# All of w_down through seven half-size products, in a two-layer encoder trunk on one core

## The chip, the core and the metric

The kernel runs on one core of a Trainium2 chip. Its time is the device time of one execution in microseconds, as the median of the runs. The profile is of one execution of its own. In it TensorE (PE) multiplies, PEld is its weight load, VectorE (DVE), ScalarE (ACT) and GpSimd (POOL) do the element-wise work, and SyncE (SP) issues most DMAs.

## The reference, cut to what matters

There are 512 tokens of width 1024, in two layers. Each layer is a mixer of attention heads, added to the residual, and then a squared-ReLU MLP, added to the residual. A final RMS norm follows. All of it is float32.

```python
def squared_relu_mlp(h, w_up, w_down):            # h 512x1024, w_up 1024x4096, w_down 4096x1024
    return jnp.square(jax.nn.relu(h @ w_up)) @ w_down

def reference(...):
    for layer in range(2):
        h = rmsnorm(x, norm_mix[layer])
        x = x + (even_mixer(h, ...) if layer == 0 else odd_mixer(h, ...))
        x = x + squared_relu_mlp(rmsnorm(x, norm_mlp[layer]), w_up[layer], w_down[layer])
    return rmsnorm(x, norm_final)
```

## The kernel before

**Precision.** A float32 matrix is split into two parts for TensorE: `hi`, a copy in fp32r made by ScalarE, and `lo`, the remainder, which VectorE makes with one subtraction. A product of two matrices is then three matmuls (`mm3`): hi by hi, hi by lo, lo by hi. Each matmul has a 128x128 stationary operand, and moves up to 512 columns into one PSUM bank.

**Order of the work.** The program text only records operations. The class `Plan` then orders them with a list scheduler. It has its own table of costs and the number of buffers of every pool. On each engine it takes, of the operations that are ready, the one that was recorded first. Work inside `nc.urgent` counts as recorded 4000 places earlier. The result is a fixed order on each engine, and an engine never passes its own next instruction. All instructions carry the same line of the program in the profile (L230, the recorder), so groups are told by the names of tiles.

**The names.** `X` are the four residual tiles, 128 tokens by 1024. `u` are feature-major activations (hi and lo). `wr` is a raw piece of weights and `wh`, `wl` are its hi and lo parts. `mm` is a PSUM bank of a plain product. `ex` is a scratch tile of 512 columns.

**The MLP (`mlp`).** The hidden width of 4096 is 32 chunks of 128. `up_pair` makes two chunks of relu(h @ w_up): 2 pieces of w_up, 48 matmuls, and one VectorE operation per chunk (`ex<-mm,rstd`). `up_raw` squares them on ScalarE into tiles `sq` (`squares`). Chunks go in groups of eight, and three groups, 24 chunks, go through `seven_products`. That is Strassen's scheme in Winograd's form: the eight chunks of activations (512 tokens by 1024) are cut in halves of tokens and of chunks, and w_down (1024 by 1024) in halves of chunks and of columns. Seven half-size products, of 24 matmuls each, take the place of eight. Sums and differences of the halves are made on VectorE in place (`into`: `sq<-sq,sq`, and `rw<-rw,rw` on the raw weights). `acts` splits an activation block into `sh`, `sl`, and `weights` splits a weight block into two pairs `wh`, `wl`. The products go to the banks `pa` (`main`) and `pb` (`second`, `third`), and `add` adds the banks to `X`. Between the products the next group's `up_raw` is recorded.

The last eight chunks do it plainly. `up_split` makes hi and lo at once, and `add_proj` multiplies them, four chunks at a time, in 96 matmuls. Its second call has `last=True` and finishes the tokens of `X[0]` and `X[1]` before those of `X[2]` and `X[3]`.

**Buffers that matter here.** Pages `sh`, `sl` come from a ring of six (`hd`), so three products' activations fit. `wh`, `wl` come from a ring of eight, so two products' weights fit. `rw` comes from a ring of nine.

**The start.** SP loads `X[0]`, the gain of the first norm as a broadcast to 128 partitions, the identity, `X[1]`, three pieces of w_in, `X[2]` and `X[3]`. `norm_T` scales the rows (`ex<-X,sm,gain`), transposes them on TensorE (`tr`) and splits them. Then `v_proj` runs 192 matmuls for the values of layer 0. 60 dummy matmuls (`warm`) run first, and 12 more after the first token tile.

**After the first MLP.** `first_of_layer_1` loads weights for the values of layer 1 in two blocks of 256 columns, partly into `hd` pages. `norm_T` follows, and then `v_proj` with 192 matmuls of 256 columns.

Of the kernel before, what the change touches and what calls it, by code (L numbers as in the profile page):

```python
# [25 lines left out]
WARM = 60  # L26
WARM2 = 12
LAYER_0 = """v a0 f0 f1 a1 a2 f2 f3 a3 f4 f5 f6 b0 f7 b1 c0 c1 b2 c2 b3 c3 x of c4 c5 c6 oc c7"""
# [356 lines left out]
def trunk(ctx, tc, x, positions, norm_mix, norm_mlp, norm_final, w_in_ab, b_forget, rel_bias,  # L385
# [56 lines left out]

    def load_w(view, parts=None, place="w", raw_place="w"):


        n = int(np.prod(view.shape[1:]))
        if raw_place == "hd":
            raw = hp.tile([P, 1024], F32, tag="hd", name=nm("wr"))
        else:
            raw = wp.tile([P, 1024], F32, tag="wr", name=nm("wr"), bufs=2)  # L450
        if place == "hd":
# [71 lines left out]
    def norm_rows(xt, g, n):  # L523

        junk = otile()
        ss = small(1)
        nc.scalar.activation(junk.bitcast(BF16)[:, :n], xt, AF.Square, accum_out=ss)
        r = rstd_of(ss, n)
        pieces = []
        for c in range(0, n, S):  # L530
            m = min(S, n - c)
            t = etile()
            nc.vector.scalar_tensor_tensor(t[:, :m], xt[:, c:c + m], r, g[:, c:c + m], ALU.mult, ALU.mult)
            pieces.append(t)
        return pieces
# [19 lines left out]

    def norm_T_(X, g_row, g=None, after=None):

        g = gain(g_row, D) if g is None else g
        hT = [(utile(), utile()) for _ in range(NC // 2)]
        for t in range(NT):  # L560
            for h, piece in enumerate(norm_rows(X[t], g, D)):
                to_feature_major(piece, 4, hT[2 * h:2 * h + 2], t)
            if t == 0 and after is not None:
                after(hT)
        return [(hi[:, k], lo[:, k]) for hi, lo in hT for k in range(2)]
# [46 lines left out]

    def col_blocks(w, kc, col, n, places=None, raw_place="w"):


        if places is None:
            per = 1024 // n
            places = [(min(per, kc - c), "w") for c in range(0, kc, per)]
        of, c = {}, 0
        for k, place in places:  # L620
            b = load_w(rows(w, c, c + k, col, col + n), place=place, raw_place=raw_place)
# [193 lines left out]

    def seven_products(X, R, wd, k0):

# [28 lines left out]

        def product(banks, A, B, first):

            for i in range(4):
                for q in range(2):  # L850
                    a = tuple(h[:, i, q * P:(q + 1) * P] for h in A)
                    b = tuple(h[:, i % 2] for h in B[i // 2])
                    mm3(banks[q], a, b, first and i == 0, i == 3, skip_group_check=not first)

        def add(banks, row, col):
            for q in range(2):
                xs = X[2 * row + q][:, col * S:(col + 1) * S]
                nc.vector.tensor_tensor(xs, banks[q], xs, ALU.add)

# [12 lines left out]
        add(second, 1, 1)  # L872
        yield

        into(a21, a22, a21, SUB)
# [9 lines left out]
        yield  # L885

        into(b11, b21, b11, SUB)
        product(second, acts(a22), weights(b11), False)
        add(second, 1, 0)
        yield  # L890

        third = side()
        product(third, acts(a12), weights(b21), True)
        add(third, 0, 0)
        yield

        into(a21, a12, a21, SUB)
        product(main, acts(a21), weights(b22), False)
        add(main, 0, 1)
        yield  # L900

    def mlp(X, g_row, wu, wd, ahead=None):

# [35 lines left out]
        def squares():  # L939
            return [up.tile([P, 2, S], F32, tag="u", name=nm("sq")) for _ in range(4)]  # L940

        R = squares()
        for pr in range(4):
            up_raw(0, pr, R)
        for g in range(3):
            steps = seven_products(X, R, wd, 8 * g)
            nxt = squares() if g < 2 else None
            act = []
            for pr, n in enumerate((2, 2, 2, 1)):
                for _ in range(n):  # L950
# [7 lines left out]
            R = nxt  # L958
        nxt = up_split(3584)
        if ahead is not None:  # L960
            ahead()
        add_proj(X, act, 4, wd, 24)
        add_proj(X, nxt, 4, wd, 28, last=True)

# [16 lines left out]
    def first_loads():  # L981
        g0.append(gain(norm_mix[0:1, :], D))
        nc.sync.dma_start(ident, consts[:, O_ID:O_ID + P])

    def first_weights():
        early[0] = {1: col_blocks(w_in_ab, NC, 1280, 264, raw_place="hd")}

    early = {}
    X = load_x(xr, between={0: first_loads, 1: first_weights})
    def keep_warm(hT):  # L990
        a = hT[0][0][:, 0, 0:P]
        for _ in range(WARM2):
            nc.tensor.matmul(warm[:, 0:P], lhsT=a, rhs=a, start=True, stop=True)

    hT = norm_T(X, None, g=g0[0], after=keep_warm)

    early[0][0] = col_blocks(w_in_ab, NC, 1024, 256)
    vw, ftail = v_proj(w_in_ab, 1024, hT, extra=8, order=(1, 0), w=early[0])
# [115 lines left out]
    def first_of_layer_1():  # L1114
        early["v"] = [col_blocks(w_in_cd, NC, 1024, 256, [(4, "hd"), (4, "hd")]),
                      col_blocks(w_in_cd, NC, 1280, 256, [(4, "hd"), (2, "rd")])]

    mlp(X, norm_mlp[0:1, :], w_up[0], w_down[0], ahead=first_of_layer_1)


# [131 lines left out]
    def step(name):  # L1252
        nonlocal vw, cq, ck, cqT, ckT, KR, o, wq, wkv
        kind, i = name.rstrip("01234567"), int(name[-1]) if name[-1].isdigit() else None
        if kind == "v":
            first, last = early["v"]
            tail = col_blocks(w_in_cd[6 * P:], 2, 1280, 256, [(2, "rd")])
            vw, _ = v_proj(w_in_cd, 1024, hT, w={0: first, 1: lambda c: last(c) if c < 6 else tail(c - 6)})
        elif kind == "q":
# [68 lines left out]
    add_proj(X, oD[2:4], 2, w_out_cd, 6, last=True)  # L1328
    mlp(X, norm_mlp[1:2, :], w_up[1], w_down[1])

# [46 lines left out]
```

## Time and profile before

| what | value |
|---|---|
| device time, median of 3 runs | 1189.9 us (1189.68 to 1191.11) |
| the profiled execution, device time | 1191.89 us |
| its span | 1190.2 us |
| PE, DVE, ACT, POOL busy in the span | 98%, 73%, 50%, 14% |
| matmuls | 5962 |

The page gives the busy time and the number of instructions of each engine. Then it gives the span in 40 slices, the DMA queues, the chain of work that ended last, and groups of like instructions with their mean duration and the idle time before them. The windows view gives busy time by stretches, with the granted clock of TensorE (PEclk). The timeline gives single instructions with start and duration in microseconds. Consecutive matmuls overlap: each is shown longer than the distance to the next.

### The profile page before, as it was taken

To read this page: it belongs to the slowest core of one execution; us is meant where nothing else is said; L and a number is where in the kernel's file an instruction comes from. 1 tells how busy PE (TensorE), PEld (TensorE's weight loads), DVE (VectorE), ACT (ScalarE), POOL (GpSimd) and SP (SyncE) were. 2 spreads that over 40 slices of the span, in tenths; PEclk is the share of its full clock that TensorE was granted. 3 is DMA by queue.
4 is the path that set the end of the run, shared out by engine and by line. 5 is a ranking of instruction groups with operands and counts; after the bars stand their busy time and mean duration, and the time that the engine had idled before them with its cause. 6 is when DMAs were issued, how large, how long until landed. Compare 5 with 4: busy or idle time off the path is not lost.

```text
span 1190.2 us, 16361 instructions
## 1 busy us (share of the span) xinstructions
PE 1168.5 (98%) x5962; PEld 990.9 (83%) x5962; DVE 864.6 (73%) x1452; ACT 596.4 (50%) x1066; POOL 168.1 (14%) x303
## 2 busy tenths in 40 slices
PE   8999999999999999999999998999999999999997
PEld 8988888788888888887898987788888888888886
DVE  6547888685977877776755879778768778687645
ACT  5347777544443444444435756566644434344423
POOL 2216522100000000000003718022100000000000
PEclk9999999999999999999999999899999999999999
DMA  6533335443143241215332230782622413321221
GB/s 200 152 94 110 93 85 169 154 156 89 36 141 107 67 146 53 71 36 172 119 105 62 60 120 30 178 226 76 213 71 71 155 58 121 109 71 36 85 92 71
DMA packets 101088, 126.85 MB, mean 107 GB/s; under 512 B 5304, under 2 KB 71232, under 8 KB 101008
## 3 DMA queue, kind: packets, MB, share of 16 engines
q1 hardware_dynamic: 100768, 125.50, 34.5%
q8 instruction: 47, 0.77, 0.2%
q0 software_dynamic: 240, 0.31, 0.2%
q14 instruction: 33, 0.27, 0.1%
HBM read 112.12 MB, written 4.23 MB: 98 GB/s over the span
## 4 chain that ended last, share of the span: by engine, by line
PE 89%; DVE 4%; DMA 4%; ACT 1%; issue 1%; POOL 0%; SPq 0%; POOLq 0%; ACTq 0%; DVEq 0%
PE mm L230 60%; PE pa L230 11%; PE pb L230 8%; PE tr L230 4%; PE sc L230 3%; PE av L230 3%; DMA KH<-KH 1%; DVE u L230 1%; DVE wl L230 1%; DMA X<-in_x_dram 1%; DVE ex L230 1%; DVE k L230 1%; ACT wh L230 1%; DMA wr<-in_w_down_dram 1%; DMA wr<-in_w_in_cd_dram 0%
## 5 line engine op out<-in xcount | busy, mean ns | idle before, releaser
L230 PE MATMUL mm<-u,wh 128*128 128x512 f32 (+1 forms) x1524 | 466.6, 384 | 1.1 <-DVE u L230 1.0
L230 PEld LDWEIGHTS mm<-u,wh 128*128 128x128 f32 x1524 | 281.1, 189 | 53.0 <-DVE u L230 1.8
L230 PE MATMUL mm<-u,wl 128*128 128x512 f32 (+1 forms) x762 | 292.5, 384 | 0.0
L230 PE MATMUL mm<-wh,u 128*128 128x512 f32 (+4 forms) x1008 | 269.6, 349 | 1.3 <-DVE o L230 0.6
L230 DVE TENSOR_TENSOR wl<-wr,wh 128x1024 fp32r<-128x1024 f32 (+5 forms) x152 | 173.8, 1149 | 74.5 <-ACT wh L230 73.7
L230 ACT CAST wh<-wr 128x1024 fp32r<-128x1024 f32 (+5 forms) x152 | 149.6, 988 | 152.3 <-PE mm L230 73.5
L230 PEld LDWEIGHTS mm<-wh,u 128*128 128x128 f32 x1008 | 176.1, 190 | 21.4 <-DVE X L230 1.2
L230 PE MATMUL mm<-wl,u 128*128 128x512 f32 (+4 forms) x504 | 175.1, 348 | 0.9 <-DVE wl L230 0.8
L230 PEld LDWEIGHTS mm<-u,wl 128*128 128x128 f32 x762 | 143.8, 189 | 26.0 <-DVE wl L230 0.2
L230 ACT CAST wh<-rw 128x1024 fp32r<-128x1024 f32 x84 | 88.5, 1054 | 114.3 <-PE mm L230 54.0
L230 DVE TENSOR_TENSOR wl<-rw,wh 128x1024 fp32r<-128x1024 f32 x84 | 102.8, 1224 | 57.0 <-ACT wh L230 56.5
L230 PEld LDWEIGHTS mm<-wl,u 128*128 128x128 f32 x504 | 95.7, 190 | 10.4 <-DVE wl L230 1.4
L230 POOL TENSOR_TENSOR sm<-sm,mhalf 128x1 f32<-128x1 f32 x28 | 20.2, 721 | 458.3 <-DVE sm L230 458.3
L230 POOL TENSOR_SCALAR p<-p,sm 128x128 f32<-128x128 f32 (+1 forms) x96 | 53.6, 558 | 175.7 <-DVE sm L230 129.9
L230 DVE TENSOR_TENSOR X<-mm,X 128x512 f32<-128x512 f32 x80 | 54.4, 687 | 28.8 <-PE mm L230 28.5
L230 PE MATMUL pa<-wl,sh 128*128 128x512 f32 x192 | 74.7, 389 | 0.0
L230 PE MATMUL pa<-wh,sl 128*128 128x512 f32 x192 | 74.7, 389 | 0.0
L230 ACT ACTIVATE sq<-ex 128x512 f32<-128x512 f32 x48 | 30.3, 631 | 88.5 <-DVE ex L230 88.5
L230 PE MATMUL pa<-wh,sh 128*128 128x512 f32 x192 | 74.4, 389 | 0.0
L230 DVE SCALAR_TENSOR_TENSOR ex<-mm,rstd 128x512 f32<-128x512 f32 x64 | 44.1, 688 | 39.5 <-PE mm L230 34.5
L230 PE MATMUL tr<-ident,p 128*128 128x128 f32 x320 | 65.6, 280 | 5.0 <-POOL p L230 3.5
L230 PE MATMUL av<-pt,u 128*128 128x128 f32 (+3 forms) x256 | 65.6, 340 | 0.0
(133 smaller groups left out, 1674.3 us busy)
## 6 DMA issues: line engine op xcount, KB each, us to landing
wr<-in_w_up_dram SPq DMA_DIRECT2D x64, 512.0 KB, 3.9
rw<-in_w_down_dram SPq DMA_DIRECT2D x48, 512.0 KB, 3.3
wr<-in_w_in_ab_dram SPq DMA_DIRECT2D x22, 512.0 KB, 3.9
wr<-in_w_down_dram SPq DMA_DIRECT2D x16, 512.0 KB, 3.3
wr<-in_w_in_cd_dram SPq DMA_DIRECT2D x11, 512.0 KB, 3.9
X<-in_x_dram SPq DMA_DIRECT2D x8, 512.0 KB, 6.3
wr<-in_w_out_ab_dram SPq DMA_DIRECT2D x8, 512.0 KB, 3.9
wr<-in_w_out_cd_dram SPq DMA_DIRECT2D x8, 512.0 KB, 3.9
```

The source lines that it names most:

```text
L230: getattr(getattr(self.nc, op.engine), op.method)(*op.args, **op.kw)
```

## The change

1. `mlp` is called with `groups=4` in both layers: the last eight chunks go through `seven_products` too, and `up_split` and `add_proj` drop out of the MLP. The fourth group's first two up pairs are recorded within the third group, the other two after the fourth's first product. In the fourth group (`last`), the product of the second row of tokens into the first columns is moved to the end, and its matmuls and those of the product before it go bank by bank (`apart`).
2. `squares` gives tiles of four chunks by 256 tokens, so each block of activations is one tile, and its sums and splits are one operation of 1024 columns in place of two of 512. The squaring writes two halves of 256.
3. The start: the gain is loaded as one row and spread by two matmuls with a row of ones into PSUM (`gn`). The pieces of w_in are loaded between the tiles of `X`. The 12 dummy matmuls go, and the next weights are held back (`late`) until the first tile is normed.
4. The values of layer 1 use weights of 512 columns: 96 matmuls of 512 columns for 192 of 256.

```diff
@@ norm_rows
-            nc.vector.scalar_tensor_tensor(t[:, :m], xt[:, c:c + m], r, g[:, c:c + m], ALU.mult, ALU.mult)
+            if isinstance(g, list):
+                nc.vector.scalar_tensor_tensor(t[:, :m], g[c // S], r, xt[:, c:c + m], ALU.mult, ALU.mult)
+            else:
+                nc.vector.scalar_tensor_tensor(t[:, :m], xt[:, c:c + m], r, g[:, c:c + m], ALU.mult, ALU.mult)
@@ seven_products(X, R, wd, k0, last=False)
-        a11, a21, a12, a22 = ([R[j + i][:, :, q:q + 256] for i in range(2)] for j in (0, 2) for q in (0, 256))
+        a11, a21, a12, a22 = ([r] for r in R)
...
+        def product(banks, A, B, first, apart=False):
+            for i, q in [(i, q) for q in range(2) for i in range(4)] if apart else [(i, q) for i in range(4) for q in range(2)]:
...
+        def second_row():
+            into(b11, b21, b11, SUB)
+            product(second, acts(a22), weights(b11), False, last)
+            add(second, 1, 0, last)
+        def first_row():
+            third = [mm_ps(), mm_ps()] if last else side()
+            product(third, acts(a12), weights(b21), True)
+            add(third, 0, 0)
...
+        if not last:
+            second_row()
+            yield
+        first_row()
         yield
+        into(a21, a12, a21, SUB)
+        product(main, acts(a21), weights(b22), False, last)
+        add(main, 0, 1, last)
         yield
+        if last:
+            second_row()
+            yield
@@ mlp
         def up_raw(g, pr, R):
             for m, r in enumerate(up_pair(1024 * g + 256 * pr, first=(g == 0 and pr == 0))):
-                nc.scalar.activation(R[pr][:, m], r, AF.Square)
+                for q in range(2):
+                    nc.scalar.activation(R[2 * (pr // 2) + q][:, 2 * (pr % 2) + m], r[:, 256 * q:256 * q + 256],
+                                         AF.Square)
...
+        for g in range(groups):
+            steps = seven_products(X, R, wd, 8 * g, last=g == 3)
+            if g == 3:
+                next(steps)
+                for pr in range(2, 4):
+                    up_raw(3, pr, R)
+                for _ in steps:
+                    pass
+                break
...
-            for pr, n in enumerate((2, 2, 2, 1)):
+            for pr, n in enumerate((3, 3) if g == 2 and groups == 4 else (2, 2, 2, 1)):
@@ the start
-        g0.append(gain(norm_mix[0:1, :], D))
+        row = utile(F32).rearrange("p a b -> p (a b)")
+        nc.sync.dma_start(row[0:1], norm_mix[0:1, :])
...
+                nc.tensor.matmul(ps, lhsT=one[0:1, 0:P], rhs=row[0:1, c * S:c * S + S], start=True, stop=True)
...
+X = load_x(xr, between={0: first_loads, 1: first_weights, 2: lambda: some_weights(6, 2)})
@@ layer 1
-    mlp(X, norm_mlp[0:1, :], w_up[0], w_down[0], ahead=first_of_layer_1)
+        early["v"] = col_blocks(w_in_cd, NC, 1024, 512, [(2, "hd"), (2, "hd"), (2, "hd"), (1, "rd"), (1, "rd")])
+    mlp(X, norm_mlp[0:1, :], w_up[0], w_down[0], ahead=first_of_layer_1, groups=4)
...
+                v_store(vw[t], token_proj(early["v"], hT, t, NC, S), 4)
```

How the order on the engines changes is shown at three places. In a row, what is left of the arrow is written. A number behind a name tells one tile of that name from another.

**VectorE, the last group of products in the MLP of layer 0.** Before (`sl_1136` and `sl_1142` are the last activation splits of the third and the fourth product; `pb` is the bank of the second):

```order
L230 TENSOR_TENSOR sl_1136<-sq_988,sh_1135 128x512
L230 TENSOR_TENSOR sq_988<-sq_988 128x2x256
L230 TENSOR_TENSOR sl_1142<-sq_987,sh_1141 128x512
L230 TENSOR_TENSOR sq_988<-sq_990,sq_988 128x2x256
L230 TENSOR_TENSOR X_638<-pb_1103,X_638 128x512
L230 TENSOR_TENSOR X_639<-pb_1104,X_639 128x512
```

Now (`mm_1203` is the bank of the group's last up chunk, `pb` that of the second product, `sl_1215` the third's split and `sl_1221` the fourth's):

```order
L229 SCALAR_TENSOR_TENSOR ex_1205<-mm_1203,rstd_845 128x512
L229 TENSOR_TENSOR wl_1219<-rw_1171,wh_1218 128x1024
L229 TENSOR_TENSOR sq_1091<-sq_1093,sq_1091 128x1024
L229 TENSOR_TENSOR wl_1223<-rw_1172,wh_1222 128x1024
L229 TENSOR_TENSOR X_641<-pb_1206,X_641 128x512
L229 TENSOR_TENSOR X_642<-pb_1207,X_642 128x512
L229 TENSOR_TENSOR sl_1215<-sq_1091,sh_1214 128x1024
L229 TENSOR_TENSOR sq_1090<-sq_1091,sq_1090 128x1024
L229 TENSOR_TENSOR wl_1225<-rw_1173,wh_1224 128x1024
L229 TENSOR_TENSOR sq_1091<-sq_1092,sq_1091 128x1024
L229 TENSOR_TENSOR sl_1221<-sq_1090,sh_1220 128x1024
```

The third and the fourth product's splits stood ahead of the second's additions to `X`; now they stand behind them. The group's last up chunk stands close ahead of them.

**ScalarE, the end of the program** (`X_1650` and `X_1661` are the last token tile, `o` takes the squares, `sm` their sums). Before:

```order
L230 ACTIVATE o_2387,sm_2388<-X_1650 128x512
L230 ACTIVATE u_2380<-u_2380,sm_2385 128x512
L230 ACTIVATE o_2387,sm_2389<-X_1650 128x512
L230 ACTIVATE u_2386<-u_2386,sm_2391 128x512
```

Now:

```order
L229 ACTIVATE u_2397<-u_2397,sm_2402 128x512
L229 ACTIVATE o_2404,sm_2406<-X_1660 128x512
L229 ACTIVATE o_2410,sm_2411<-X_1661 128x512
L229 ACTIVATE u_2403<-u_2403,sm_2408 128x512
L229 ACTIVATE o_2410,sm_2412<-X_1661 128x512
L229 ACTIVATE u_2409<-u_2409,sm_2414 128x512
```

The rows are the same for the last tile. The half of `X_1661` that the last product writes is now the first half (the row with `sm_2411`); before it was the second (the row with `sm_2389`).

**VectorE, the start** (`ex_127` and `ex_130` are the first scaled pieces). Before:

```order
L230 TENSOR_SCALAR sm_125<-sm_124 128x1
L230 SCALAR_TENSOR_TENSOR ex_127<-X_101,sm_126,gain_102 128x512
L230 SCALAR_TENSOR_TENSOR ex_128<-X_101,sm_126,gain_102 128x512
L230 TENSOR_SCALAR sm_133<-sm_132 128x1
L230 TENSOR_TENSOR u_116<-tr_129,u_115 128x2x128
```

Now:

```order
L229 TENSOR_SCALAR sm_128<-sm_127 128x1
L229 TENSOR_TENSOR wl_108<-wr_106,wh_107 128x792
L229 SCALAR_TENSOR_TENSOR ex_130<-gn_104,sm_129,X_101 128x512
L229 SCALAR_TENSOR_TENSOR ex_131<-gn_105,sm_129,X_101 128x512
L229 TENSOR_SCALAR sm_136<-sm_135 128x1
L229 TENSOR_TENSOR wl_112<-wr_110,wh_111 128x792
```

A split of w_in, and with it the wait for its load, has come ahead of the first scaled piece.

More of the change, by code (lines that the diff above doesn't have):

```diff
@@ L441, in mm3, with load_w @@
         nc.tensor.matmul(ps, lhsT=a[1], rhs=b[0], start=False, stop=last, **kw)
-    def load_w(view, parts=None, place="w", raw_place="w"):
+    def load_w(view, parts=None, place="w", raw_place="w", late=None):
         n = int(np.prod(view.shape[1:]))
@@ L450, in load_w @@
             raw = wp.tile([P, 1024], F32, tag="wr", name=nm("wr"), bufs=2)
+        if late is not None:
+            mark(raw, late)
         if place == "hd":
@@ L620, in col_blocks @@
         for k, place in places:
-            b = load_w(rows(w, c, c + k, col, col + n), place=place, raw_place=raw_place)
+            b = load_w(rows(w, c, c + k, col, col + n), place=place, raw_place=raw_place, late=late)
             for i in range(k):
@@ L845, in into, with add @@
                 nc.vector.tensor_tensor(o, p, q, op)
[L847 to L855, printed above, removed]
+        def product(banks, A, B, first, apart=False):
+            for i, q in [(i, q) for q in range(2) for i in range(4)] if apart else [(i, q) for i in range(4) for q in range(2)]:
+                a = tuple(h[:, i, q * P:(q + 1) * P] for h in A)
+                b = tuple(h[:, i % 2] for h in B[i // 2])
+                mm3(banks[q], a, b, first and i == 0, i == 3, skip_group_check=not first)
+        def add(banks, row, col, final=False):
             for q in range(2):
                 xs = X[2 * row + q][:, col * S:(col + 1) * S]
-                nc.vector.tensor_tensor(xs, banks[q], xs, ALU.add)
+                if final or not (False):
+                    nc.vector.tensor_tensor(xs, banks[q], xs, ALU.add)
+                else:
+                    t = sp.tile([P, S], F32, tag="p3", name=nm("xa"))
+                    nc.scalar.copy(t, banks[q])
+                    nc.gpsimd.dma_start(xs, t, accum_op=ALU.add)
         SUB, ADD = ALU.subtract, ALU.add
@@ L885, in seven_products, with mlp @@
         yield
[L887 to L894, printed above, removed]
+        if not last:
+            second_row()
+            yield
+        first_row()
         yield
         into(a21, a12, a21, SUB)
-        product(main, acts(a21), weights(b22), False)
-        add(main, 0, 1)
+        product(main, acts(a21), weights(b22), False, last)
+        add(main, 0, 1, last)
         yield
-    def mlp(X, g_row, wu, wd, ahead=None):
+        if last:
+            second_row()
+            yield
+    def mlp(X, g_row, wu, wd, ahead=None, groups=3):
         hT, rstd = gained_T(X, g_row)
@@ L939, in squares @@
         def squares():
-            return [up.tile([P, 2, S], F32, tag="u", name=nm("sq")) for _ in range(4)]
+            return [up.tile([P, 4, 256], F32, tag="u", name=nm("sq")) for _ in range(4)]
         R = squares()
@@ L981, in first_loads, with some_weights @@
     def first_loads():
-        g0.append(gain(norm_mix[0:1, :], D))
+        row = utile(F32).rearrange("p a b -> p (a b)")
+        nc.sync.dma_start(row[0:1], norm_mix[0:1, :])
         nc.sync.dma_start(ident, consts[:, O_ID:O_ID + P])
+        one = etile()
+        nc.vector.memset(one[0:1, 0:P], 1.0)
+        for c in range(2):
+            ps = ps_sc.tile([P, S], F32, tag="sc", name=nm("gn"))
+            with nc.urgent(BOOST):
+                nc.tensor.matmul(ps, lhsT=one[0:1, 0:P], rhs=row[0:1, c * S:c * S + S], start=True, stop=True)
+            g0.append(ps)
+        some_weights(0, 3)
+    first_of = {}
+    def some_weights(c, k):
+        b = load_w(rows(w_in_ab, c, c + k, 1280, 1544), raw_place="hd")
+        for i in range(k):
+            first_of[c + i] = tuple(h[:, i] for h in b)
     def first_weights():
-        early[0] = {1: col_blocks(w_in_ab, NC, 1280, 264, raw_place="hd")}
+        some_weights(3, 3)
+        early[0] = {1: first_of.get}
     early = {}
[L989 to L997, printed above, removed]
+    X = load_x(xr, between={0: first_loads, 1: first_weights, 2: lambda: some_weights(6, 2)})
+    hT = norm_T(X, None, g=g0)
+    early[0][0] = col_blocks(w_in_ab, NC, 1024, 256, late=f32(hT[0][0][:, P:P + 1]))
     vw, ftail = v_proj(w_in_ab, 1024, hT, extra=8, order=(1, 0), w=early[0])
@@ L1255, in step @@
         if kind == "v":
-            first, last = early["v"]
-            tail = col_blocks(w_in_cd[6 * P:], 2, 1280, 256, [(2, "rd")])
-            vw, _ = v_proj(w_in_cd, 1024, hT, w={0: first, 1: lambda c: last(c) if c < 6 else tail(c - 6)})
+            vw = []
+            for t in range(NT):
+                vw.append(utile().rearrange("p a b -> p (a b)").rearrange("p (a n) -> p a n", n=256))
+                v_store(vw[t], token_proj(early["v"], hT, t, NC, S), 4)
         elif kind == "q":
@@ L1328, in trunk @@
     add_proj(X, oD[2:4], 2, w_out_cd, 6, last=True)
-    mlp(X, norm_mlp[1:2, :], w_up[1], w_down[1])
+    mlp(X, norm_mlp[1:2, :], w_up[1], w_down[1], groups=4)
     g = gain(norm_final, D)
```

23 lines of the change are left out of this document (9 added, 14 removed).

## The prediction

> **What bounds the kernel now.** I read the page's busy shares first, then the windows view for the stages that the change touches, then the chain of waits for the pace of the matmuls.
>
> ```profile
> PE 1168.5 (98%) x5962; PEld 990.9 (83%) x5962; DVE 864.6 (73%) x1452; ACT 596.4 (50%) x1066; POOL 168.1 (14%) x303
> ```
>
> ```profile
> core 0: us, PE busy (x) PEld busy (x) DVE busy (x) ACT busy (x) POOL busy (x), PEclk, DMA share, GB/s
> ...
> 555.00:556.00 1.00, 0.30 (x1) 0.00 (x0) 1.00 (x2) 0.00 (x0) 0.00 (x0) 1.00 0.60 231
> 308.60:390.00 81.40, 81.40 (x361) 67.41 (x360) 63.21 (x75) 35.03 (x44) 0.00 (x0) 1.00 0.33 104
> ```
>
> ```profile
> 308.63 5.44 PE pa L230 x24
> 314.07 5.44 PE pb L230 x24
> 319.51 10.88 PE mm L230 x48
> ```
>
> TensorE is the bound. In a whole group of seven products with its up chunks (308.6 to 390.0) it has no idle time, at full clock, while VectorE is busy 63.2 of 81.4 us. Its pace is 5.44/24 = 0.2267 us per matmul of 512 columns. A matmul less in this stage is 0.2267 us less, as long as VectorE keeps up.
>
> **A, the matmuls.** The plain last eight chunks are 2 x 96 = 192 matmuls per layer; seven products are 7 x 24 = 168. Over both layers that is 384 less and 336 more: 48 x 0.2267 = -10.9 us. This is certain as long as TensorE stays the bound.
>
> **B, the values of layer 1.**
>
> ```profile
> 605.76 0.28 PE L230 MATMUL mm<-wl,u 128*128 128x256 f32 x1
> 605.88 0.40 PE L230 MATMUL mm<-wh,u 128*128 128x256 f32 x2
> 606.12 0.28 PE L230 MATMUL mm<-wl,u 128*128 128x256 f32 x1
> ```
>
> Three matmuls of 256 columns start in 0.36 us, so each takes 0.120. 192 x 0.120 = 23.0 go and 96 x 0.2267 = 21.8 come: -1.3 us (rounding kept). The Trainium skill (TensorE: Matmul & The Clock Gate, "Wait — 56ns, not 53.3ns?") gives columns divided by 2.4 GHz plus 2.5 ns, so two of 256 would cost only 2.5 ns more than one of 512. By that the gain would be 0.2 us, and the sum 1.1 us less good. The rows have 13 ns per pair, and I go by them.
>
> **C, the start.**
>
> ```profile
> 6.67 1.42 DVE L230 SCALAR_TENSOR_TENSOR ex<-X,sm,gain 128x512 f32<-128x512 f32 x2 [0.69 <-POOL sm L230]
> ...
> 8.90 1.06 ACT L230 ACTIVATE o<-X 128x1024 bf16<-128x1024 f32 x1 [3.11 <-DMA X<-in_x_dram]
> ...
> 24.73 0.74 DVE L230 TENSOR_TENSOR u<-tr,u 128x256 fp32r<-128x256 f32 x2
> ```
>
> ```profile
> 5.00:6.00 1.00, 1.00 (x15) 1.00 1.04 212
> 6.00:7.00 1.00, 0.82 (x15) 1.00 0.83 202
> 7.00:8.00 1.00, 0.52 (x4) 1.00 0.96 372
> ```
>
> ```profile
> 7.00:25.50 18.50, 10.24 (x66) 0.91 0.61 220
> ```
>
> The first and second fences are the timeline and the windows view (last column GB/s); the third is the windows view of the tile `mm` alone. While the gain is broadcast the DMA moves 202 to 212 GB/s, otherwise 372. Without those 512 KB, every later load lands 2 to 3 us earlier. Against that, the first scaled piece must now wait behind a split of w_in, whose load comes right after `X[0]`. I put that load at 5.7, ScalarE's cast at 6.9, the split at 7.9 and the first piece there: 1.3 us later than 6.67. From the second tile on VectorE is the limit in both. Adding up its rows in the new order, the last token tile is split at 24.6, against 25.5 before. At 25.5 TensorE had done 66 of the 192 matmuls of the values, so 126 were left; the new order has 79 ahead of that point, so 113 are left. The gain is 0.9 + 13 x 0.12 = 2.5 us: **-2.5**. Bounds: -3.5 (all of the earlier landing), and +1.5 (the first piece's delay runs through to the end). The 12 dummy matmuls that go stood in idle time. Their cover is the clock, which fell to 0.57 between 12 and 16 us even with them (row below), where TensorE waits for VectorE.
>
> **D, VectorE in the fourth group.** Its cost per instruction:
>
> ```profile
> L230 DVE TENSOR_TENSOR wl<-rw,wh 128x1024 fp32r<-128x1024 f32 x84 | 102.8, 1224 | 57.0 <-ACT wh L230 56.5
> ...
> L230 ACT CAST wh<-rw 128x1024 fp32r<-128x1024 f32 x84 | 88.5, 1054 | 114.3 <-PE mm L230 54.0 <-PE pa L230 33.2 <-PE pb L230 27.1
> ...
> L230 DVE SCALAR_TENSOR_TENSOR ex<-mm,rstd 128x512 f32<-128x512 f32 x64 | 44.1, 688 | 39.5 <-PE mm L230 34.5 <-issue 4.2
> ```
>
> ```profile
> 519.27 1.22 DVE L230 TENSOR_TENSOR wl<-rw,wh 128x1024 fp32r<-128x1024 f32 x1
> 520.40 1.28 DVE L230 TENSOR_TENSOR X<-pb,X 128x512 f32<-128x512 f32 x2
> 521.69 1.23 DVE L230 TENSOR_TENSOR wl<-rw,wh 128x1024 fp32r<-128x1024 f32 x1
> ```
>
> An operation of 1024 lasts 1.22 us, but the next may start 1.13 after it; two of 512 take 1.28. So back to back they cost 1.13 and 0.60. A full product needs 3 sums, 3 splits and 2 additions to `X`: 6 x 1.13 + 2 x 0.60 = 8.0 us of VectorE for 5.44 us of TensorE. In the first three groups up chunks fill the difference. In the fourth, all remaining up chunks run between the first and the second product, and six products follow without a break. VectorE must therefore work ahead, within the rings of pages.
>
> I count from the end of the fourth group's first product. 93 up matmuls fill TensorE until 21.1. Then, by the order shown: `ex` 21.3; `wl` 22.0; the difference of the activations needs the squares of that `ex` and starts at 23.1; the next `wl` needs a page which the second product frees halfway (23.8) and a cast of 1.05, so 25.2; the additions wait for the second product's end (26.5), so 26.6 and 27.2; `sl` of the third product 27.8 to 29.0. TensorE begins the third product at 26.5, has four matmuls without `sl`, and waits from 27.4 to 29.0: 1.6 us. Carried on, the fourth product's `sl` ends at 33.6, just when the third ends, and later operands are 1 to 3 us early. Two layers: **+3.3** (1.65 each). Bounds: 0 (the additions turn out not to be in the way), and 4.3 (each operation at its full duration: 29.4 for the start of the rest, 2.15 each).
>
> **E, from the first MLP to layer 1.** Before, the row of 555 to 556 shows the one hole, 0.7 us, where `add_proj` waited for weights. It goes. Carrying the count on, `X[0]` is complete at 48.8 and the last product ends at 55.4. VectorE first has the last product's and two more weight splits, additions and the angles of the rotary keys in its queue, so the first normed piece starts at 54.7. TensorE transposes it at 55.6. ScalarE has a weight cast before the hi copy, and the values begin at 57.2: 1.3 us without work, then no more. Together **+0.6**. Bounds: -0.7 (no new hole), +3.3 (VectorE at full durations: 4.0 without work).
>
> **F, the end.**
>
> ```profile
> 1182.72 0.39 PE L230 MATMUL mm<-wh,u 128*128 128x512 f32 x1
> ...
> 1183.15 0.69 DVE L230 TENSOR_TENSOR X<-mm,X 128x512 f32<-128x512 f32 x1 [1.08 <-PE mm L230]
> ...
> 1183.88 0.63 ACT L230 ACTIVATE o<-X 128x512 bf16<-128x512 f32 x1 [0.42 <-DVE X L230]
> ...
> 1184.97 0.55 POOL L230 TENSOR_TENSOR sm<-sm,mhalf 128x1 f32<-128x1 f32 x1 [2.27 <-DVE sm L230]
> 1185.55 0.72 ACT L230 ACTIVATE u<-u,sm 128x512 f32<-128x512 f32 x1 [0.96 <-POOL sm L230]
> 1185.56 0.75 DVE L230 SCALAR_TENSOR_TENSOR u<-X,sm,gain 128x512 f32<-128x512 f32 x1 [0.73 <-POOL sm L230]
> ```
>
> Before, the last addition starts as the last matmul ends (1183.11), and the scaling ends 3.2 us after it. Now VectorE comes to the last addition 0.3 us late. ScalarE then squares the new half, scales the tile before (which waits for its own `sm`), and only then squares the other half, although that was ready long ago. By these rows the scaling ends 5.6 us after the last matmul: **+2.4**. Bounds: 0 and 3.5.
>
> **At nothing.** Squaring in two halves costs ScalarE more, and joined operations save VectorE some; in the first three groups both lie beside a TensorE that is never idle (row of 308.6). If VectorE fell behind there too, it would be D again. SP issues 16 w_down loads into `rw` in place of 16 into `wr`, ahead of the up loads as before; the DMA share there is 0.33.
>
> **Sum:** -10.9 - 1.3 - 2.5 + 3.3 + 0.6 + 2.4 = -8.4 us. The span goes from 1190.2 to 1181.8. The median was 1189.9; the profiled execution was 2.0 above it. I take the difference off the median: **1181.5 us**.
>
> **Rivals.**
>
> 1. VectorE without overlap of its operations. 4.3, 3.3 and 3.5 stand for D, E and F: -3.6, 1186.3 us. For it: new waits lie between many of these operations. Against: the rows at 519 to 522 are of just this mixture. Chance 0.18.
>
> 2. The start gains nothing (C at +1.5), because the row of ones waits for its own load and two matmuls before the first piece: -4.4, 1185.5 us. Chance 0.12. With rival 1 on top it is +0.4, 1190.3 us: chance 0.07.
>
> 3. Slower: the granted clock falls in the new holes.
>
> ```profile
> 736.00:740.00 4.00, 2.49 (x12) 1.40 (x11) 3.97 (x7) 2.97 (x6) 2.70 (x6) 0.95 0.00 0
> 740.00:744.00 4.00, 2.26 (x10) 1.46 (x9) 3.99 (x5) 0.58 (x1) 3.12 (x2) 0.50 0.02 4
> 744.00:748.00 4.00, 3.85 (x10) 2.74 (x11) 3.34 (x6) 1.08 (x2) 0.00 (x0) 0.50 0.58 100
> 748.00:752.00 4.00, 4.00 (x18) 3.50 (x17) 2.04 (x4) 1.91 (x4) 0.00 (x0) 0.77 0.80 180
> 12.00:16.00 4.00, 3.48 (x16) 3.31 (x17) 3.44 (x9) 2.75 (x7) 0.55 (x1) 0.57 1.02 375
> ```
>
> There the clock lost (0.05 + 0.50 + 0.50 + 0.23) x 4 = 5.1 us. One such fall in each of the three holes (the two of D, that of E) is 15.4: +7.0, 1196.9 us. Two falls give 1191.7, so it decides from three. Against: the hole of 0.7 us at 555 left the clock at 1.00, and mine are 1.3 to 1.65, alone between dense work. Chance 0.06. The Trainium skill (same page, "The HAM clock gate") says that the clock halves after an idle window of about 3.4 us; by that none of my holes brings it down, and this rival is worth nothing. The trace does not bear that out: it fell at 736 to 744 with TensorE shown busy over half of the time.
>
> **Chances and range.** The forecast has 0.57. Anything under 0.2% (2.4 us) cannot be told from no change: 1187.5 to 1192.3. Faster: the forecast, rival 2 and nearly all of rival 1, with some loss from their own spread: 0.80. Same: 0.13, slower: 0.07. The bounds together reach from 1175.3 to 1193; all at one end is unlikely, so I take 1176.5 to 1189.
>
> **What would show it.** A: 336 matmuls into `pa`, `pb` and `mm<-wh,sh` more, at 5.44 us for 24. C: the 192 matmuls of the values end some 2.5 us earlier, and no load of 512 KB stands before `X[1]`. D: a wait of 1.6 us for `sl` in the third product of each fourth group, and hardly another. E: the first `tr` of layer 1 behind the last `pb`, with a hole of about 1.3 us. F: 5 to 6 us from the last matmul to the last scaling. I am wrong if the holes in D are several, if PEclk falls below 1.00 in the MLPs, or if the layers' heads, which the change does not touch, move by more than 2 us.

## The result, and the profile after

The changed kernel takes 1182.4 us (median of 6 runs, 1181.8 to 1183.1). The kernel before, run beside it, takes 1190.3. The ratio is 0.9932, with a 95% interval of 0.9922 to 0.9943: 7.9 us less, give or take 1.3. The profiled execution has a span of 1180.1 us, against 1190.2.

The page of the changed kernel, first part:

```profile
PE 1154.1 (98%) x5810; PEld 973.1 (82%) x5810; DVE 899.8 (76%) x1415; ACT 614.5 (52%) x1094; POOL 169.7 (14%) x303
```

TensorE has 14.4 us less to do, and VectorE 35 more. TensorE is still the bound. The chain of waits of the changed kernel, second MLP, from the last group's first product to the end:

```profile
1110.73 5.44 PE pa L229 x24
1116.17 21.08 PE mm L229 x93
1137.25 2.51 PE pb L229 x11
1140.87 1.22 DVE wl L229
1142.09 1.33 DVE X L229 x2
1143.41 1.14 DVE sl L229
1144.60 4.87 PE pa L229 x20
1149.93 5.56 PE pa L229 x24
1155.49 4.99 PE mm L229 x22
1160.47 5.44 PE pa L229 x24
1165.91 5.45 PE pb L229 x24
```

The seven products and the up chunks at full pace would take 7 x 5.44 + 21.08 = 59.16 us. From 1110.73 to 1171.36 they take 60.63. Most of the 1.47 us of difference lies where the chain leaves TensorE: it goes through VectorE's `wl`, the additions to `X` and `sl`, as in the prediction's term D. The waits of TensorE, changed kernel (in total, times, longest):

```profile
PE tr L229 <- DVE ex L229: 2.7, 1, 2.7
PE pa L229 <- DVE sl L229: 2.0, 2, 1.0
...
PE mm L229 <- ACT u L229: 1.3, 1, 1.3
```

The first is at the start (C), the second is D in both layers, the third is the hole at the hand-over to layer 1 (E).

**Where the time went.** I cut each profile at five rows of TensorE: the first scores (`sc<-KH,Q`) of layer 0, the first `pb` of each MLP, the first scores of layer 1, and the last matmul's end. Each number is one of these starts less the one ahead of it, in us. The last column is what remains of the span. "Again" is a second profile of the same kernel, and the other names are those of the experiments below.

| profile | start to scores 0 | to MLP 0 | MLP 0, values, to scores 1 | to MLP 1 | MLP 1 to last matmul | after it |
|---|---|---|---|---|---|---|
| before | 80.1 | 233.8 | 325.9 | 260.3 | 283.0 | 7.1 |
| before, again | 79.8 | 233.4 | 325.0 | 259.3 | 283.0 | 7.1 |
| changed | 79.4 | 232.3 | 321.2 | 259.3 | 279.1 | 8.7 |
| changed, again | 81.4 | 232.5 | 321.7 | 258.6 | 279.1 | 8.8 |
| start only | 79.7 | 232.3 | 325.0 | 258.6 | 283.1 | 7.1 |
| values only | 80.3 | 233.4 | 324.8 | 259.2 | 283.0 | 7.0 |
| MLPs only | 80.2 | 233.4 | 332.8 | 259.3 | 279.1 | 8.8 |
| MLPs and values | 79.7 | 233.5 | 320.7 | 259.5 | 279.1 | 8.8 |

The fifth column does not move between executions of one kernel. It says that an MLP gains 4.0 us net (before rounding). Two of the differences between the first two profiles belong to the execution: the 0.8 us hole at 555 us and a deeper fall of the clock at 736 to 752 us are not in the second profile of the kernel before.

### The profile page after: what moved, and what is told of

Its sections match the earlier page's. It is cut to its first block, busy times and chain, and to the rows that moved or that the text cites. A ratio compares the mean times of both kernels' runs of the same rounds, so it can differ in the third digit from the quotient of the medians.

```text
span 1180.1 us, 16054 instructions
## 1 busy us (share of the span) xinstructions
PE 1154.1 (98%) x5810; PEld 973.1 (82%) x5810; DVE 899.8 (76%) x1415; ACT 614.5 (52%) x1094; POOL 169.7 (14%) x303
## 4 chain that ended last, share of the span: by engine, by line
PE 88%; DVE 5%; issue 3%; DMA 2%; POOL 1%; ACT 1%; SPq 0%; POOLq 0%; DVEq 0%; ACTq 0%
PE mm L229 55%; PE pa L229 14%; PE pb L229 9%; PE tr L229 4%; PE sc L229 3%; PE av L229 3%; DVE wl L229 1%; DVE k L229 1%; DMA wr<-in_w_in_ab_dram 1%; POOL p L229 1%; DVE u L229 1%; DVE ex L229 1%; DVE X L229 1%; ACT wh L229 1%; DVE pt L229 1%
## 5 line engine op out<-in xcount | busy, mean ns | idle before, releaser
L229 DVE TENSOR_TENSOR wl<-rw,wh 128x1024 fp32r<-128x1024 f32 x112 | 136.4, 1221 | 72.8 <-ACT wh L229 72.6
L229 PE MATMUL mm<-wh,u 128*128 128x512 f32 (+4 forms) x704 | 188.2, 347 | 2.5 <-ACT u L229 1.3
L229 ACT CAST wh<-rw 128x1024 fp32r<-128x1024 f32 x112 | 117.9, 1053 | 134.6 <-PE mm L229 62.2
L229 PEld LDWEIGHTS mm<-wh,u 128*128 128x128 f32 x704 | 121.7, 190 | 14.8 <-ACT u L229 1.6
L229 PE MATMUL mm<-wl,u 128*128 128x512 f32 (+4 forms) x352 | 120.8, 344 | 0.4 <-DVE wl L229 0.4
L229 ACT ACTIVATE sq<-ex 128x256 f32<-128x256 f32 x128 | 46.4, 409 | 132.3 <-DVE ex L229 132.3
L229 PE MATMUL pa<-wh,sh 128*128 128x512 f32 x256 | 99.5, 390 | 0.0
L229 DVE TENSOR_TENSOR rw<-rw,rw 128x1024 f32<-128x1024 f32 x64 | 77.9, 1220 | 0.8
L229 PEld LDWEIGHTS mm<-wl,u 128*128 128x128 f32 x352 | 67.0, 191 | 5.5 <-DVE wl L229 0.6
L229 PE MATMUL pb<-wh,sl 128*128 128x512 f32 x176 | 68.5, 389 | 0.0
```

Of the source, the lines that this page charges most:

```text
L229: getattr(getattr(self.nc, op.engine), op.method)(*op.args, **op.kw)
```

## The experiments

### Each part alone

`e1_mlp_only` keeps the start and the values of layer 1 as before, `e2_start_only` and `e3_v512_only` make one of the other parts alone, and `e4_before_again` is the kernel before. The edits are the hunks of the diff above:

```diff
e1: mlp(..., groups=4), seven_products(..., last), squares() by halves of the tokens   -- and nothing else
e2: gn by a row of ones, w_in between the tiles of X, late=, no WARM2                   -- and nothing else
e3: early["v"] = col_blocks(w_in_cd, NC, 1024, 512, ...), one token_proj of 512         -- and nothing else
```

> Only the change in the two MLPs (all 32 chunks of w_down in seven products, four square tiles by halves of the tokens); the start and the values of layer 1 as before. The prediction's terms A, D and F give -10.9 + 3.3 + 2.4 = -5.2 us against the kernel before, and so about 1185. My reading of the two traces gives A -10.9, D +2.9, F +1.7, so -6.3, and up to 0.6 less if the hole of term E at the hand-over to layer 1 belongs to the MLP and not to the values. Rival: if the 1.4 us that the heads of layer 0 and the stall at 736 to 752 us differ by between the two profiles were an effect of the change and not of the execution, this kernel, whose start is as before, would gain 1 to 2 us more than that or show the same shift in its profile.

> Only the change at the start (gain by a product with a row of ones, the w_in pieces loaded between the tiles of x, no 12 extra products); MLPs and values as before. The prediction's term C says -2.5 us (bounds -3.5 to +1.5). The trace of the changed kernel says -0.65: VectorE holds the first scaled piece until 9.99 us, behind the split of a w_in piece that lands at 8.2. If the 1.4 us wait for KH at about 205 us goes away with the start, -2.1; if that wait is of the execution, -0.65.

> Only the values of layer 1 as 96 matmuls of 512 columns in place of 192 of 256. Term B from the rows of this case: -1.3 us (192 x 0.120 against 96 x 0.2267); by the formula of the Trainium skill's TensorE page the gain would be 0.2. If the hole of 1.3 us at the hand-over belongs to the values' new weight pieces, that hole shows here too and the time is within 0.7 of no change.

> The kernel before once more, unchanged, for a second profile. If the wait of TensorE for KH at about 205 us (1.4 us in the first profile) and the clock's fall at 736 to 752 us are parts of this program, they are there again with the same sizes; if they belong to one execution, one or both are missing or of another size, and the 1.5 us between this kernel's profiled 1191.9 and its median 1190.3 go with them.

Measured against 1190.3 us: MLPs only 1196.8 (ratio 1.0051, 1.0039 to 1.0064), slower, where the expectation was 5 to 6 us less. Start only 1189.4 (0.9993, 0.9984 to 1.0002). Values only 1190.2 (0.9999, 0.9990 to 1.0008). Alone, the three parts add up to +5.4 us, and together they give -7.9. I had added them up as independent terms; they are not.

The table shows the place: MLP 1 and the end are as in the changed kernel, but the stretch with the hand-over takes 332.8 us. Timeline of TensorE (and the row of VectorE that its last wait names) and windows view of "MLPs only" (busy time of each engine, then PEclk, DMA share and GB/s):

```profile
592.50 0.60 PE L230 MATMUL tr<-ident,ex 128*128 128x128 f32 x4
...
598.36 0.60 PE L230 MATMUL tr<-ident,ex 128*128 128x128 f32 x4
...
603.12 0.60 PE L230 MATMUL tr<-ident,ex 128*128 128x128 f32 x4
...
608.75 0.60 PE L230 MATMUL tr<-ident,ex 128*128 128x128 f32 x4
610.22 0.66 PE L230 MATMUL tr<-ident,ex 128*128 128x128 f32 x4 [0.87 <-DVE ex L230]
615.43 0.55 PE L230 MATMUL mm<-wh,u 128*128 128x256 f32 x1 [4.56 <-DVE u L230]
...
614.88 1.07 DVE L230 TENSOR_TENSOR u<-mm,u 128x256 fp32r<-128x256 f32 x3
```

```profile
590.00:600.00 10.00, 7.96 (x51) 6.57 (x49) 9.20 (x19) 6.07 (x14) 3.44 (x6) 1.00 0.69 228
600.00:610.00 10.00, 7.78 (x62) 7.28 (x62) 8.66 (x19) 4.56 (x12) 0.00 (x0) 1.00 0.22 64
610.00:612.00 2.00, 0.66 (x4) 0.42 (x4) 1.83 (x6) 1.10 (x4) 0.00 (x0) 1.00 0.26 51
612.00:618.00 6.00, 2.56 (x12) 2.60 (x13) 5.89 (x13) 2.01 (x3) 0.00 (x0) 0.50 0.41 107
```

The same stretch in the changed kernel, and in the kernel before:

```profile
590.00:600.00 10.00, 8.67 (x46) 7.02 (x45) 8.68 (x18) 5.74 (x15) 3.03 (x5) 1.00 0.65 221
600.00:610.00 10.00, 10.00 (x53) 8.26 (x52) 9.09 (x20) 4.79 (x12) 0.00 (x0) 1.00 0.28 83
```

```profile
600.00:610.00 10.00, 10.00 (x86) 9.97 (x85) 8.48 (x18) 5.97 (x14) 0.81 (x2) 1.00 0.65 218
```

VectorE is busy 8 to 10 us of every 10 in all of them. In "MLPs only" TensorE starves beside it, again and again, and at last for 4.6 us. This last wait is not for a transpose: it ends with `u<-mm`, in which VectorE empties finished banks of the values, and which on VectorE stands behind the angles of the rotary keys. The clock falls to 0.50 for over 6 us: the mechanism of the prediction's rival 3, in a hole that the changed kernel does not have. The Trainium skill (TensorE: Matmul & The Clock Gate, "The HAM clock gate") ties such a fall to an idle window of about 3.4 us. Here the clock is down from 612, 1.1 us into the hole of 4.6 (from 610 to 612 TensorE was busy for a third): a shorter fully idle time than the page's.

### Order or width of the values

`e9_mlp_and_v512` adds the wide values to "MLPs only". `e10_v256_by_tile` is the changed kernel with narrow matmuls in the new order:

```diff
+ps = mm_ps()
+for q in (0, 256):
+    for c in range(NC):
+        mm3(ps[:, q:q + 256], <tokens of tile t>, <256 columns of w>, c == 0, c == NC - 1)
-v_store(vw[t], token_proj(early["v"], hT, t, NC, S), 4)
+v_store(vw[t], ps, 4)
```

> The MLP part and the values at 512 columns together, the start as before. Alone they gave +6.5 and -0.1 us. If the hand-over to layer 1 is what made the MLP part slow alone (TensorE waiting there for VectorE, 4.6 us at once, and the clock falling in it) and the wide values close it, then this is A + B + D + E + F with a start worth about -1.0 missing: 1183 to 1184 us, ratio 0.994 to 0.995. If the start also has a part in closing it, more than 1186.

> The changed kernel, but each token tile's values in two halves of 256 columns, one after the other in the same bank (192 matmuls as before, and in the new order: all 512 columns of a tile before the next tile). Theory 1, the order counts: a tile's products last as long as VectorE and ScalarE take over the next one, so only the narrower matmuls cost, +1.3 us (192 x 0.120 against 96 x 0.2267) against the changed kernel, 1183 to 1184. Theory 2, it is the width of the matmuls that counts (as in the term B of the prediction, and more): much of the 13 us by which the MLP part alone was slower comes back, over 1187.

Measured: MLPs and values 1183.0 us (0.9940, 0.9929 to 0.9952). Narrow values by tile 1184.9 (0.9958, 0.9946 to 0.9969). So the values turn "MLPs only" from +6.5 to -7.3 us, and the start has no part in it. In the hand-over's column the narrow values by tile have 323.7 us, against 332.8 for "MLPs only" and 321.2 for the changed kernel: 9.1 us by the order (with the sizes of the weight pieces, which differ too), 2.5 by the width. Theory 1 holds, though its 1.3 us for the width was too little. The pace of the narrow matmuls is as in the rows of the prediction: 15 of them take 1.80 us (599.16 to 600.96). TensorE also waits for VectorE twice (0.23 us at 596.0, 0.24 at 597.8) where the changed kernel does not wait. What the rest of the 2.5 is, is open.

My reading of it: in blocks of 256 columns a token tile's products last 24 x 0.12 = 2.9 us. In "MLPs only" the next tile's transposes come 5 to 6 us apart (592.5, 598.4, 603.1, 608.8). All 512 columns of a tile last 5.4 us and nearly fill that. Before, the plain chunks finished `X[0]` and `X[1]` half a call ahead of the end, so the first tiles were normed in time. That last sentence is argued from the order, not tried.

### Term D: VectorE in the last group

`e5_defer_add` puts the second product's additions behind the third product's split; `e5b_split_first` holds back two more kinds of sums (`one` is a factor of 1 read from the split):

```diff
 product(second, acts(a21), weights(b12), True)
-add(second, 1, 1)
+if not last:
+    add(second, 1, 1)
 ...
+a = acts(a21)
+nc.vector.tensor_scalar(one, f32(a[1][:, 0, 0:1]), 0.0, 1.0, ALU.mult, ALU.add)
+nc.vector.scalar_tensor_tensor(xs, second[q], one, xs, ALU.mult, ALU.add)     # e5 and e5b, q = 0, 1
+nc.vector.scalar_tensor_tensor(o, p, one, q, ALU.mult, op)                    # e5b: sums for a11 and for second_row's b11
```

> The changed kernel, with the two additions of the second product of the last group put behind the split of the third product's activations on VectorE (by a factor of one that is read from that split; one small operation more). Term D: the wait of TensorE for sl in the third product, 1.0 us in both layers in the profile, is VectorE being late by these two additions (1.3 us), so it goes: -2.0 us in all, up to -2.9 if the small gap before the fourth product goes with it; 1179.5 to 1180.5. Rival: the lateness has been there since the squares and sums ahead of it and the additions push only what comes after: the wait stays within 0.3 of 1.0, or turns up at the fourth product, and the time within 0.5 of the changed kernel's.

> The changed kernel with three things held back in the last group until the split of the third product's activations is done on VectorE: the second product's two additions, the sum that makes the fourth product's activations, and the sums for the second row's weights. On VectorE the split then stands directly behind the square sum it needs. Theory D as in the prediction (VectorE comes late to this one split): the wait of 1.0 us goes in both layers, -2 us. Rival, which e5 suggests: VectorE has work without a gap from there to the fourth product, so what is held back makes the fourth product late: the wait at the third product falls to under 0.3, one of 0.8 to 1.3 us turns up at the fourth, and the time is within 0.7 of the changed kernel's.

Measured: 1182.2 us (0.9934, 0.9921 to 0.9946), no gain; and 1185.2 (0.9950, 0.9937 to 0.9962), 2 to 3 us worse than the changed kernel. ScalarE and VectorE in the last group, changed kernel, then VectorE in `e5_defer_add`, with TensorE's wait there, then `e5b_split_first`:

```profile
1134.39 1.05 ACT L229 CAST wh<-rw 128x1024 fp32r<-128x1024 f32 x1 [1.10 <-PE mm L229]
...
1135.47 1.22 DVE L229 TENSOR_TENSOR wl<-rw,wh 128x1024 fp32r<-128x1024 f32 x1 [2.94 <-ACT wh L229]
...
1140.87 1.22 DVE L229 TENSOR_TENSOR wl<-rw,wh 128x1024 fp32r<-128x1024 f32 x1
1142.05 1.37 DVE L229 TENSOR_TENSOR X<-pb,X 128x512 f32<-128x512 f32 x2
1143.33 1.22 DVE L229 TENSOR_TENSOR sl<-sq,sh 128x1024 fp32r<-128x1024 f32 x1
```

```profile
1142.03 1.22 DVE L229 TENSOR_TENSOR sq<-sq,sq 128x1024 f32<-128x1024 f32 x1
1143.16 1.22 DVE L229 TENSOR_TENSOR sl<-sq,sh 128x1024 fp32r<-128x1024 f32 x1
...
1144.44 0.74 PE L229 MATMUL pa<-wh,sl 128*128 128x512 f32 x2 [0.82 <-DVE sl L229]
```

```profile
1142.71 1.22 DVE L229 TENSOR_TENSOR sl<-sq,sh 128x1024 fp32r<-128x1024 f32 x1
...
1149.02 1.28 DVE L229 TENSOR_TENSOR X<-pa,X 128x512 f32<-128x512 f32 x2
...
1149.85 0.47 PE L229 MATMUL pa<-wh,sh 128*128 128x512 f32 x1 [1.03 <-DVE X L229]
```

In e5 the scheduler had another sum ready for the freed place, and `sl` came 0.17 us earlier. In e5b `sl` stands free and TensorE hardly waits for it (0.2 us in all), but it waits 1.0 us in each layer at the fourth product, for the additions that read the third product's banks. MLP 1 takes 279.5 us in place of 279.1, and the span ends 11.1 us after the last matmul in place of 8.8. The rival has the waits right, though not the time, which it put within 0.7 of the changed kernel's. From 1135.5 to the fourth product the changed kernel's profile shows no wait of VectorE, so the loss of 1.5 us per layer is not the place of two additions.

A rival stays untested. Just before, VectorE stood idle for 2.94 us, until ScalarE had cast a piece of weights; the cast itself had waited for TensorE's up matmuls, which, as I read it, still held the page that it writes (the ring of eight). With more pages, or another order of the casts, some of VectorE's work could come earlier. No run tries this.

### Term F: the end

`e6_tail_new_half_last`, for the last two token tiles of the final norm:

```diff
-junk = otile().bitcast(BF16)
+junk = (otile() if t < 2 else etile()).bitcast(BF16)
+if t >= 2: sa, sb, v, r = the columns of a tile of their own
+A, B = (slice(S, D), slice(0, S)) if t >= 2 else (slice(0, S), slice(S, D))
```

> The changed kernel, with the final norm of the last two token tiles squaring first the half of the columns that is done early (products two and four of the last group), with small tiles and scratch of its own so that this can start early. Term F: 4.9 us from the last matmul to the last scaling, of which ScalarE spends two operations of 0.6 us and a scaling of 0.72 of the tile before that could not start earlier. If F is that queue on ScalarE, the tail is 3.2 to 3.8 us and the time 1.1 to 1.7 us less than the changed kernel's. Rival: the chain add, square, mean, power, scaling alone sets it, and the gain is under 0.4.

Measured: 1182.0 us (0.9927, 0.9915 to 0.9939), which cannot be told from the changed kernel. ScalarE at the end of the changed kernel, where the last matmul ends at 1171.35:

```profile
1172.18 0.63 ACT L229 ACTIVATE o<-X 128x512 bf16<-128x512 f32 x1 [0.31 <-DVE sm L229]
...
1173.25 0.72 ACT L229 ACTIVATE u<-u,sm 128x512 f32<-128x512 f32 x1 [0.35 <-POOL sm L229]
1173.88 0.61 ACT L229 ACTIVATE o<-X 128x512 bf16<-128x512 f32 x1
...
1175.50 0.72 ACT L229 ACTIVATE u<-u,sm 128x512 f32<-128x512 f32 x1 [0.92 <-POOL sm L229]
```

and of `e6_tail_new_half_last`, where it ends at 1172.63:

```profile
1173.39 0.63 ACT L229 ACTIVATE ex<-X 128x512 bf16<-128x512 f32 x1 [0.51 <-DVE X L229]
...
1174.75 1.33 ACT L229 ACTIVATE u<-u,sm 128x512 f32<-128x512 f32 x2 [0.64 <-POOL sm L229]
```

VectorE's last scaling ends at 1176.25 in the changed kernel, 4.9 us after the last matmul, and at 1176.17 here, 3.5 us after it. So ScalarE's queue was the cause, as the prediction put it. But both last tiles are now scaled at once, and the span ends 8.1 us after the last matmul in place of 8.7: half of the 1.4 us is lost behind the scaling, where only the stores of the output are left. `e8_start_and_tail` below, which has the same edit, ends 8.0 us after it.

### Term C: the start

What held the start in the changed kernel (ScalarE, VectorE, TensorE, in turn):

```profile
8.21 0.85 ACT L229 CAST wh<-wr 128x792 fp32r<-128x792 f32 x1 [2.63 <-DMA wr<-in_w_in_ab_dram]
...
9.09 0.98 DVE L229 TENSOR_TENSOR wl<-wr,wh 128x792 fp32r<-128x792 f32 x1 [3.33 <-ACT wh L229]
9.99 1.40 DVE L229 SCALAR_TENSOR_TENSOR ex<-gn,sm,X 128x512 f32<-128x512 f32 x2
...
4.57 1.98 PE L229 MATMUL gn<-u,ex 1*128 1x512 f32 x4
6.48 1.57 PE L229 MATMUL warm<-idle 128*128 128x128 bf16 x25
10.79 1.88 PE L229 MATMUL tr<-ident,ex 128*128 128x128 f32 x8 [2.75 <-DVE ex L229]
```

`e7_split_after_scaling` makes that split wait for the scaled pieces, `e8_start_and_tail` adds the edit of e6, and `e11_after_again` is the changed kernel:

```diff
+def split(piece):                       # called in norm_T_ after the first tile's scaling
+    nc.vector.tensor_copy(lo[:, 0:1], piece[:, 0:1])
+    nc.vector.tensor_tensor(lo[:, :n], raw[:, :n], f32(hi[:, :n]), ALU.subtract)
...
```

> The changed kernel once more, unchanged, for a second profile and as the reference of the three kernels run beside it. Ratio 0.992 to 0.9945 again. If the waits on which the terms rest belong to the program, the profile shows them again: TensorE waiting 1.0 us for sl in both layers, the hole of 1.3 us at the hand-over, 4.9 us from the last matmul to the last scaling, and no wait over 1 us for KH at about 205 us.

> The changed kernel, with the split of the first w_in piece made to follow the first scaled pieces of x on VectorE (a one-column copy from the second scaled piece into the split's tile). Term C was -2.5 and came out at about -0.6. Theory 1: what held the start is VectorE's order, in which this split, whose piece lands only at 8.2 us, stands ahead of the first scaling (9.99 us); now the scaling starts at 6.6, the first transposes at about 7.4 in place of 10.8, and the first product 0.8 to 1.5 earlier; this much is gained at 80 us too, 1181 to 1181.6. Theory 2: the late tiles of x and pieces of w_in set the start (X[1] lands at 9.5): the first transposes come earlier, but what follows by about 20 us is where it was, and the time is the same within 0.4.

> The edit at the start (split behind the scaling) and the edit of the final norm together on the changed kernel. If both gain what they show alone (the tail 4.9 to 3.5 us; the start by theory 1 0.8 to 1.5), 1179.5 to 1180.5 and a ratio of 0.990 to 0.992 against the kernel before; if the start gives nothing, 1181 and the same as the tail's edit alone.

Measured, beside 1191.1 us for the kernel before: changed again 1182.6 (0.9929, 0.9917 to 0.9942), split after scaling 1182.0 (0.9926, 0.9914 to 0.9939), start and tail 1183.1 (0.9930, 0.9916 to 0.9943). All the same. Theory 1 did not come about: the transposes are not earlier. TensorE in `e7_split_after_scaling`, and VectorE's second scaled piece:

```profile
4.93 3.78 PE L229 MATMUL gn<-u,ex 1*128 1x512 f32 x4
8.64 2.85 PE L229 MATMUL warm<-idle 128*128 128x128 bf16 x25
11.28 1.81 PE L229 MATMUL tr<-ident,ex 128*128 128x128 f32 x8
...
8.75 0.75 DVE L229 SCALAR_TENSOR_TENSOR ex<-gn,sm,X 128x512 f32<-128x512 f32 x1 [0.87 <-PE gn L229]
```

Here the product with the row of ones and the dummy products behind it hold the start, at little more than half the pace of the execution above. By chance `e5_defer_add`, whose start is that of the changed kernel, has the same pace in its profile (25 dummy products in 2.85 us), so it shows what the edit does there. VectorE's first scaled pieces and TensorE's first transposes in it:

```profile
9.97 1.41 DVE L229 SCALAR_TENSOR_TENSOR ex<-gn,sm,X 128x512 f32<-128x512 f32 x2
...
11.28 1.91 PE L229 MATMUL tr<-ident,ex 128*128 128x128 f32 x8
```

The transposes start at 11.28 with the edit and without it, so at this pace the split does not hold them. What follows is later with the edit: the second token tile is scaled at 16.0 in place of 14.6, and the first scores come at 81.2 us in place of 79.7. At the pace of the changed kernel's own profile, where the split does hold the first piece, the edit has no profile, so theory 1 stays open there. No edit here beats the changed kernel.

What the start does gain lies elsewhere. In all five profiles with the old start TensorE waits 0.9 to 1.4 us for `KH` in layer 0, at about 210 us, and in none of the nine with the new one does this wait show. Kernel before, and MLPs and values:

```profile
210.07 0.33 PE L230 MATMUL sc<-KH,Q 128*128 128x128 f32 x1 [1.39 <-DMA KH<-KH]
```

```profile
209.39 0.33 PE L230 MATMUL sc<-KH,Q 128*128 128x128 f32 x1 [1.09 <-DMA KH<-KH]
```

It is the 1.1 us in the column "to MLP 0" (233.4 to 233.8 against 232.2 to 232.6), whatever the start before it took. Why the new order spares it is open.

## Why the prediction was right or wrong

The forecast was 1181.5 and the time 1182.4. By terms:

- **A** (-10.9): right. Each product takes 5.44 us on TensorE, as counted.
- **D** (+3.3): right place, a little large: 60.63 - 59.16 = 1.47 us in the second MLP, and a wait of 1.0 us for `sl` in both layers, so +2.9. (The step counts 0.60 us for an addition to `X`; its own row, 520.40 to 521.69, has 1.29 for two.) The bound at 0, "the additions turn out not to be in the way", was the right doubt for another reason: without them the next sums are.
- **E** (+0.6): the new hole is right, 1.3 us in the profile (1.8 in the second one). The 0.7 us that the step took off for the hole at 555 us are not there in the second profile of the kernel before; against that one E is +1.3. What the step did not say is what keeps the hole so small: the wide values. With the old ones the hand-over costs 12 us more.
- **B** (-1.3): wrong as a term of its own. The step "192 x 0.120 go and 96 x 0.2267 come" priced the width and passed over the order, which the same edit turns from block by block to tile by tile. Alone the edit gives -0.1, give or take 1.1. In that profile TensorE waits 0.8 us for weight parts in the MLP, which the second profile of the kernel before does not; so it is not shown that the -1.3 is missing, only that it does not reach the time. With the new MLP it is worth 12 to 14 us. Undoing the width alone costs 2.5 us, of which the pace of the matmuls, 0.120 us, is the 1.3 of the step. By the formula of the Trainium skill (TensorE: Matmul & The Clock Gate, "Wait — 56ns, not 53.3ns?") the width would cost 0.2 us; the trace does not agree.
- **C** (-2.5): wrong. The failed step is "I put that load at 5.7, ScalarE's cast at 6.9, the split at 7.9 and the first piece there". The load let the cast start at 8.2, the split at 9.1, the piece at 10.0. Ahead of it stood "Without those 512 KB, every later load lands 2 to 3 us earlier". In the changed kernel the DMA falls too, without the broadcast, to 192 GB/s from 4 to 5 us and 126 from 5 to 6, and `X[1]` is used at 9.5 in place of 8.9. So the fall was not the broadcast's alone; what it is, is open. VectorE splits the last token tile at 27.2, not 24.6. The first scores of layer 0 come at 79.4 to 81.4 us with the new start and at 79.7 to 80.3 with the old: nothing gained there, the outcome of rival 2 but not its cause, since the wait is for the load and not for the row of ones. The 1.1 us that is gained stands in the heads of layer 0, which I had named as untouched; that part is luck.
- **F** (+2.4): right mechanism, in the order predicted on ScalarE; the last scaling ends 4.9 us after the last matmul in place of the 5.6 predicted, against 3.2 before, so +1.7.
- **The sum:** -10.9 + 2.9 + 1.7 - 1.1, and +0.2 for B and E together (321.2 - 325.0 = -3.8 us in that column, of which -4.0 is the MLP), is -7.2, against 7.9 measured, give or take 1.3. The forecast of -8.4 was near it because C, and B and E together, taken too well by 1.4 and 0.9 us, were set off in part by D and F, taken too badly by 0.4 and 0.7. So A, D and F were right by their mechanism, and the closeness of the whole is partly luck. The bounds of the terms add up to 1173.5 and 1190.3, not to 1175.3 and 1193 as the prediction has it.
- **Rivals.** Rival 1 falls: D and F came out under their forecast, E's hole at it, and operations of 1.22 us start 1.13 apart (1142.03 and 1143.16 above), so VectorE's operations do overlap. Rival 3 falls for this change, since its holes stay under 2 us and the clock stays at 1.00 in the MLPs and at the hand-over, but "MLPs only" shows that such a fall lay one edit away.

## What to carry to other kernels

When a change has several parts, ask of each whether it covers a hole that another one opens; price the whole at the hand-over where they meet, and undo one part at a time, because alone a part may be worth nothing and without it the rest a loss. Where a wait ends on an engine that has no gap left around it, moving one operation away from there only moves the wait. A start that is costed from when a load might land needs a row for that landing, and a second execution.

## What the runs showed of the hardware

TensorE's pace in the first 12 us differs between executions of the same instructions. 25 dummy products of 128 columns take 1.57 us in the changed kernel's profile and 2.85 in those of e5, e7 and e8, and one of the four `gn` matmuls 0.59 or 1.06, while PEclk reads 1.00 from 4 to 10 us in both. The Trainium skill (TensorE: Matmul & The Clock Gate, "The HAM clock gate") states that the first 3.4 us or so run at half rate and that this varies by run; the half pace up to 11.4 us is far longer than that. PEclk itself differs as well. In the second profile of the changed kernel and in that of e6 it is at 0.50 to 0.58 from 12 to 18 us, and the first scores come at 81.4 and 81.3 us. In the first profile it is back at 0.91 from 14 to 16, and they come at 79.4. "MLPs only", with the old start, has the long fall too, and its first scores come at 80.2, no later than others with that start. So one profile says little about a start.
